# Clipped differences on GpSimd, a split scratch array in DRAM, and four projection banks beside three scan banks

## The chip, the cores and the metric

The kernel runs on one core of a Trainium2 chip. A core has TensorE (PE in the profile; its weight loads are PEld), VectorE (DVE), ScalarE (ACT), GpSimd (POOL) and SyncE (SP, which here only issues DMAs), each with its own queue that is worked off in order. They share an SBUF of 128 partitions; TensorE writes its products to the eight banks of PSUM, 2 KB a partition each. The metric is the device time of one execution in microseconds, the median of three runs.

## The reference, cut to what matters

Two layers of a streaming encoder run over 256 frames of a new stream and 64 frames of a running one, 320 columns in all. The first layer is a Mamba-2 mixer and a convolutional feed-forward block, the second an MLA mixer and another such block. The change touches the mixer of the first layer alone, and there the scan:

```python
da = dtc * a                                   # log decay of each step, 32 heads
acs = jnp.cumsum(da, axis=2)                   # running sums in a chunk
seg = acs[:, :, :, None] - acs[:, :, None]     # l minus s
decay = jnp.exp(jnp.where(causal, seg, -jnp.inf))
cb = jnp.einsum('bclgn,bcsgn->bclsg', cc, bc)
wts = cb[..., None] * decay * dtc[:, :, None]
y_diag = jnp.einsum('bclsge,bcsgep->bclgep', wts, xc)
decay_end = jnp.exp(acs[:, :, -1:] - acs)
states = jnp.einsum('bclgn,bclge,bclgep->bcgepn', bc, decay_end * dtc, xc)
chunk_decay = jnp.exp(acs[:, :, -1])
y_off = jnp.einsum('bclgn,bcgepn,bclge->bclgep', cc, h_prev, jnp.exp(acs))
```

`seg` is at most 0 where it is used (l at or behind s), since the running sums fall; elsewhere `cb` is set to zero.

## The kernel before

Activations lie transposed: features on the partitions, the 320 columns along a row. A projection is a sum over eight blocks of 128 input features, and each product is made of three matmuls (`mm3`, lines 283 and 284), since weights and inputs are split into a high part and a rest to keep float32 precision: ScalarE writes the high part of a weight tile `wh` (line 326), VectorE the rest `wl` (line 328). Weight tiles of 512 KB come in by SP through three buffers `wr` (line 191); four split pairs may stand ready.

The mixer's input projection is 41 output blocks of 128 rows. The first four (`outer`) are multiplied with the input not yet normalized; TensorE sums the squares meanwhile, VectorE makes 1/rms (`newton`), TensorE spreads it over the partitions (line 369), ScalarE copies it (`xr`, line 388), and the four results are multiplied with it as they are copied from PSUM (lines 818 and 642). Three more blocks are treated likewise, then GpSimd multiplies the input by 1/rms (`normalized`, line 478) and the rest is projected from that. Block results lie in PSUM tiles `pm`, from a pool `m` of five banks; the small products of the scan in `px`, from a pool `x` of two; sums of squares in `pr`, one bank (`PSM`, line 47).

A block is either a convolution block (b, c or x), copied to `ext` by ScalarE (line 640), with pads put in and last rows saved by GpSimd (lines 636, 637, 643, 644) and the filter on ScalarE and VectorE (lines 647, 649), or a gate block z, copied to `sz` (line 735).

The scan works in chunks of 128, 128 and 64 columns (c = 0, 1, 2) and four groups of eight heads (g). `ssm_dt` makes the running sums `acs`, 96 rows (32 heads in three chunks) of 128, and `ssm_dt2` stores them in DRAM as `acd` (line 841), to read them back spread over the partitions. For each group `ssd_fetch` issues per chunk a load of eight rows to all 128 partitions (`dc`, line 861) and, for c > 0, two loads of four rows to 64 partitions each (`ea`, line 866). Then come 24 steps `head(c, h)`: ScalarE replaces the row of head h by the clipped difference, a Relu of the column's own sum (from `dtt`) minus the row (line 874); the first step of chunks 1 and 2 also copies the sums' last column (`cd`, line 873). `ssd_decay` takes the exponentials of `cd`, `dc` and `ea` (line 673), with the sign turned for `dc`. `ssd_steps` makes the products: `pre` (b and c, lines 903 to 909: the mask, and `dc` times it), `xpose` (x turned, line 915, and times dt, line 922), `diag` (line 932 on `dc`, line 940 on the state, copied at line 934 or added up at 942 and 943) and `states` (line 949). Each takes one or two banks of `px`.

What sets the order: `PLAN` lists projections and scan parts in the order in which they are traced. `fetch` hands its 24 steps to a list from which a pace (6 or 8) is taken after each projection block, and `decay` works off what is left. Around that the framework's planner orders the instructions of each engine by a simulated timeline, first traced first where several are ready, and sets the semaphores; on the chip the order is fixed. Extra edges keep exponentials and silus apart on ScalarE (`exp` and `silu`), since each change of function loads a table, and put the loads of `acd` behind a projection block (`issue`). The last steps of the scan run beside the output projection (`square_part`), which holds four `pm` banks at a time.

Of the kernel before, what the change touches and what calls it, by code (L numbers as in the profile page):

```python
# [11 lines left out]
AF = mybir.ActivationFunctionType  # L12
ALU = mybir.AluOpType
# [3 lines left out]
P = 128  # L17
# [26 lines left out]
PSA = dict(m=5, x=3)  # L44
PSF = dict(m=7, r=1)
PSL = dict(m=7, r=1)
PSM = dict(m=5, x=2, r=1)
XC = ((0, 128), (128, 128), (259, 64))

RSU = 0.7235248917065753  # L50
# [35 lines left out]
class Kern:  # L86
# [513 lines left out]
    def run(self):  # L600
# [4 lines left out]
        self.pst = None  # L605
        self.psum(**PSM)
        self.vec = self.t(cp, [P, VEC["_n"][0]], "vec")
# [69 lines left out]
    def ssm(self):  # L677
        nc, a = self.nc, self.a
        self.silus, self.exps, self.burst = [], [], []
        self.yg, self.dc, self.ea = {}, {}, {}  # L680
        with ExitStack() as st:
            dr = st.enter_context(self.tc.tile_pool(name="acd", bufs=1, space=bass.MemoryType.DRAM))
            self.acd = self.t(dr, [96, P], "acd")
            ap = self.pool(st, "ssma")
            ah = self.t(ap, [P, 16, T], "ah", F32R)
            al = self.t(ap, [P, 16, T], "al", F32R)
            with ExitStack() as s2:
# [4 lines left out]
                with ExitStack() as s3:  # L692
# [3 lines left out]
                    for k in range(KD):  # L696
                        r = self.raw[k] = self.t(dp, [P, 512], "w0", bufs=KD)
# [76 lines left out]
            for half in range(2):  # L774
                w = [self.nextw(), self.nextw()]
                for n in range(4):
                    m = 4 * half + n
                    if m > 3:
                        self.early_step(early)
                    p = ps[3] if m == 7 else self.px()  # L780
                    for kb in range(12, 16):
# [4 lines left out]
                        q = slice((kb % 2 * 4 + n) * 128, (kb % 2 * 4 + n) * 128 + 128)  # L786
# [50 lines left out]
    def ssm_dt2(self, dt2, sp, dp):  # L837
        nc = self.nc
        dt, acs, w = dt2

        self.issue(nc.sync.dma_start(out=self.acd, in_=acs))
        self.cd = self.t(sp, [P, 3, 32], "cd")
        for p, n in ((slice(0, 64), 128), (slice(64, 96), 64)):
            self.exp(w[p, 0:n], acs[p, 0:n], scale=-1.0, bias=acs[p, n - 1:n])
        nc.vector.tensor_tensor(out=w, in0=w, in1=dt, op=ALU.mult)
        pd = self.px()
        for i, t_ in enumerate((dt, w, acs)):
            nc.tensor.transpose(pd[:, 96 * i:96 * i + 96], t_, self.ident[0:96, 0:96])
        self.dtt = self.t(sp, [P, 288], "dtt")
        nc.vector.tensor_copy(out=self.dtt, in_=pd[:, 0:288])  # L850

    def ssd_fetch(self, g, sp):

        nc = self.nc
        self.dc[g], self.ea[g] = {}, {}

        def load():
            for c, (_, n) in enumerate(CHUNKS):
                r0 = 32 * c + 8 * g
                dc = self.dc[g][c] = self.t(sp, [P, 8, n], f"dc{c}", bufs=DCB)  # L860
                self.issue(nc.sync.dma_start(out=dc, in_=self.acd[r0:r0 + 8, 0:n].partition_broadcast(P)))
                if c > 0:
                    ea = self.ea[g][c] = self.t(sp, [P, 4, n], f"ea{c}", bufs=DCB)
                    for odd in range(2):
                        r = r0 + 4 * odd
                        self.issue(nc.sync.dma_start(out=ea[64 * odd:64 * odd + 64], in_=self.acd[r:r + 4, 0:n].partition_broadcast(64)))

        def head(c, h):
            n = CHUNKS[c][1]
            dc = self.dc[g][c]  # L870
            q = 32 * c + 8 * g + h
            if c and h == 0:
                nc.vector.tensor_copy(out=self.cd[:, c, 8 * g:8 * g + 8].unsqueeze(2), in_=dc[:, :, n - 1:n])
            nc.scalar.activation(out=dc[:n, h, :], in_=dc[:n, h, :], func=AF.Relu, scale=-1.0, bias=self.dtt[:n, 192 + q:193 + q])  # L874

        return load, [lambda c=c, h=h: head(c, h) for c in range(3) for h in range(8)]

    def ssd_decay(self, g):

        cd = self.cd[:, 1:3, 8 * g:8 * g + 8]  # L880
        self.exp(cd, cd)
        for c, (_, n) in enumerate(CHUNKS):
            dc = self.dc[g][c]
            self.exp(dc[:n], dc[:n], scale=-1.0)
            if c > 0:
                self.exp(self.ea[g][c], self.ea[g][c])

# [624 lines left out]
```

## Time and profile before

| what | value |
|---|---|
| median of 3 runs | 1002.08 us (999.59 to 1002.16) |
| the profiled execution | 1002.07 us, span 1000.3 us |
| mean granted clock of TensorE | 0.983 |
| ScalarE, line 874 | 96 instructions, 28.3 us busy |
| loads `dc` / `ea` | 12 / 16 DMAs |
| the first layer's mixer | the first 260 us or so |

The span is the time from the first instruction to the last; the profiled execution's own time has 1.8 us around it. In rows of a timeline the columns are the start in us, the duration in us, engine, line, operation and operands (out<-in), how many instructions were merged, and in brackets the idle time before and what ended it. In rows of stretches the columns are the stretch, its length, each engine's busy time with the number of its instructions, the granted clock, the busy share of the DMA engines and GB/s. In rows for one line three numbers stand for the least, the median and the longest duration in ns. In rows of DMA issues the last two numbers are KB each and the median time from issue to landing in us.

### The profile page before, as it was taken

What the parts mean: (1) busy time and instruction counts of PE and PEld (TensorE: products, weight loads), DVE (VectorE), ACT (ScalarE), POOL (GpSimd) and SP (SyncE); (2) the same over time, 40 slices, a digit from 0 to 9 for tenths busy, and PEclk for the clock granted to TensorE, in tenths of its full rate; (3) what the DMA queues carried; (4) which work ended last, traced back from release to release, by engine and by line L of the source; (5) the groups of instructions that cost most, each with busy time, mean ns of one, the idle gap of its engine ahead of it and who ended that gap; (6) DMA issues with size and microseconds to landing.
All of it is one profiled execution on the core that took longest, in us unless ns stands there. A gap on an engine that the chain in (4) does not pass through costs nothing.

```text
span 1000.3 us, 18088 instructions
## 1 busy us (share of the span) xinstructions
PE 960.9 (96%) x6585; PEld 930.1 (93%) x6585; DVE 746.7 (75%) x1425; ACT 620.4 (62%) x1285; POOL 337.1 (34%) x597
## 2 busy tenths in 40 slices
PE   8897999999999999999999999999999999999995
PEld 7897999979989999999998899999999999999994
DVE  7865888887677998784538898886538999775433
ACT  6589797833555687664544677775544778664330
POOL 3921321100044775430005765530004766441001
PEclk9998999999999999999999999999999999999998
DMA  7374637353324444455641222233443455444531
GB/s 262 108 213 143 211 125 224 115 172 90 117 74 141 156 150 158 156 157 178 194 139 35 86 67 69 56 106 98 148 145 96 136 170 168 149 144 143 151 116 53
DMA packets 50905, 135.54 MB, mean 136 GB/s; under 512 B 11488, under 2 KB 15232, under 8 KB 50816
## 3 DMA queue, kind: packets, MB, share of 16 engines
q1 hardware_dynamic: 50528, 134.06, 42.6%
q8 instruction: 51, 0.84, 0.4%
q14 instruction: 38, 0.31, 0.1%
q10 hardware_dynamic: 288, 0.33, 0.1%
HBM read 130.25 MB, written 4.12 MB: 134 GB/s over the span
## 4 chain that ended last, share of the span: by engine, by line
PE 80%; DVE 9%; ACT 5%; POOL 3%; issue 2%; DMA 1%; SPq 0%; POOLq 0%; ACTq 0%; DVEq 0%
PE pm L283 46%; PE pm L284 23%; PE px L283 2%; PE px L932 1%; ACT wh L326 1%; PE px L949 1%; PE px L284 1%; POOL xacc L442 1%; PE pr L362 1%; PE px L940 1%; ACT dc L874 1%; DVE wl L328 1%; POOL xn L478 1%; DVE y L450 1%; DVE x L454 1%
## 5 line engine op out<-in xcount | busy, mean ns | idle before, releaser
L326 ACT ACTIVATE wh<-wr 128x1024 fp32r<-128x1024 f32 (+4 forms) x235 | 228.0, 973 | 160.0 <-PE pm L283 141.9
L328 DVE TENSOR_TENSOR wl<-wr,wh 128x1024 fp32r<-128x1024 f32 (+2 forms) x204 | 244.2, 1197 | 110.4 <-ACT wh L326 109.3
L283 PE MATMUL pm<-xnh,wh 128*128 128x320 f32 x784 | 243.4, 312 | 3.9 <-ACT xnh L329 3.2
L283 PE MATMUL pm<-xnl,wh 128*128 128x320 f32 x784 | 244.6, 312 | 0.3 <-DVE xnl L330 0.3
L284 PE MATMUL pm<-xnh,wl 128*128 128x320 f32 x784 | 243.4, 311 | 0.0
L283 PEld LDWEIGHTS pm<-xnh,wh 128*128 128x128 f32 x784 | 147.5, 189 | 6.5 <-ACT xnh L329 3.8
L284 PEld LDWEIGHTS pm<-xnh,wl 128*128 128x128 f32 x784 | 147.8, 189 | 1.7 <-issue 1.7
L283 PEld LDWEIGHTS pm<-xnl,wh 128*128 128x128 f32 x784 | 147.9, 189 | 1.3 <-issue 0.7
L283 PE MATMUL pm<-ah,wh 128*128 128x320 f32 x452 | 139.8, 311 | 1.7 <-ACT ah L329 1.7
L284 PE MATMUL pm<-ah,wl 128*128 128x320 f32 x452 | 140.6, 311 | 0.0
L283 PE MATMUL pm<-al,wh 128*128 128x320 f32 x452 | 140.4, 311 | 0.0
L649 DVE SCALAR_TENSOR_TENSOR cv<-ext,vec,cv 128x322 f32<-128x322 f32 x176 | 96.7, 563 | 5.4 <-ACT cv L647 3.0
L636 POOL MEMSET ext<- 128x2 f32 (+1 forms) x112 | 10.8, 98 | 245.9 <-DVE al L330 83.2
L643 POOL COPY fsave<-ext 128x2 f32<-128x2 f32 x88 | 72.5, 823 | 53.6 <-ACT ext L640 49.3
L283 PEld LDWEIGHTS pm<-ah,wh 128*128 128x128 f32 x452 | 84.7, 188 | 2.5 <-ACT ah L329 2.0
L283 PEld LDWEIGHTS pm<-al,wh 128*128 128x128 f32 x452 | 85.1, 188 | 1.0 <-issue 1.0
L284 PEld LDWEIGHTS pm<-ah,wl 128*128 128x128 f32 x452 | 85.1, 188 | 1.0 <-issue 1.0
L328 POOL TENSOR_TENSOR wl<-wr,wh 128x512 fp32r<-128x512 f32 (+2 forms) x31 | 43.6, 1424 | 102.3 <-ACT wh L326 100.9
L283 PE MATMUL pm<-xgl,wh 128*128 128x320 f32 x220 | 68.3, 314 | 1.0 <-DVE xgl L426 1.0
L284 PE MATMUL pm<-xgh,wl 128*128 128x320 f32 x220 | 68.2, 313 | 0.7 <-DVE wl L330 0.7
L283 PE MATMUL pm<-xgh,wh 128*128 128x320 f32 x220 | 62.5, 316 | 2.8 <-ACT wh L329 1.3
L647 ACT ACTIVATE cv<-ext,vec 128x322 f32<-128x322 f32 x88 | 57.1, 654 | 9.5 <-POOL ext L637 6.6
(395 smaller groups left out, 2132.4 us busy)
## 6 DMA issues: line engine op xcount, KB each, us to landing
wr<-w_up SPq DMA_DIRECT2D x76, 512.0 KB, 3.3
wr<-w_in SPq DMA_DIRECT2D x37, 512.0 KB, 3.7
wr<-w_dn SPq DMA_DIRECT2D x32, 512.0 KB, 3.6
wr<-w_out SPq DMA_DIRECT2D x16, 512.0 KB, 3.4
wr<-w_o SPq DMA_DIRECT2D x16, 512.0 KB, 3.4
wr<-w_up_k SPq DMA_DIRECT2D x16, 384.0 KB, 3.2
wr<-w_dn SPq DMA_DIRECT2D x16, 384.0 KB, 3.2
dc<-acd SPq DMA_DIRECT2D x8, 512.0 KB, 6.4
```

Source lines behind the costliest of these rows:

```text
L283: for i in (mm(out, wh, xh, start=first, stop=False), mm(out, wh, xl, start=False, stop=False), mm(out, wl, xh, start=False, stop=last)):
L284: mm(out, wl, xh, start=False, stop=last)):
L326: self.high_ins = nc.scalar.activation(out=hdst, in_=src, func=AF.Copy).ins
L328: return lambda: e.tensor_tensor(out=ldst, in0=src, in1=hdst.bitcast(F32), op=ALU.subtract)
L362: i = self.nc.tensor.matmul(ps[:, o + b:o + b + 1], acc[:, l0:l0 + 128], self.ones[:, 0:1], start=True, stop=True)
L442: nc.gpsimd.tensor_tensor(out=acc, in0=acc, in1=s, op=ALU.add)
L450: tt(out=yk, in0=yk, in1=r, op=ALU.mult)
L454: e.tensor_tensor(out=xk, in0=xk, in1=yk, op=ALU.add)
L636: nc.gpsimd.memset(ext[:, 0:m], 0.0)
L643: nc.gpsimd.tensor_copy(out=rows_out[:, 0, :], in_=ext[:, TP:TP + m])
L647: nc.scalar.activation(out=c, in_=ext[:, 0:n], func=AF.Identity, scale=w(0), bias=b)
L649: nc.vector.scalar_tensor_tensor(out=c, in0=ext[:, i:i + n], scalar=w(i), in1=c, op0=ALU.mult, op1=ALU.add)
```

## The change

Three edits. The difference of a head is made on GpSimd with one tensor_scalar (the row minus the column's own sum, then the minimum with zero) in place of the Relu on ScalarE; its sign is turned, so the exponential of `dc` takes no scale. The scratch array in DRAM becomes two: chunks 0 and 1 in 64 rows of 128, chunk 2 in 32 rows of 64, stored by two DMAs; each load reads its rows as one run and writes each partition's tile as one run. The pool `m` has four banks and the pool `x` three.

```diff
-PSM = dict(m=5, x=2, r=1)
+PSM = dict(m=4, x=3, r=1)
...
-            self.acd = self.t(dr, [96, P], "acd")
+            self.acd = self.t(dr, [64, P], "acd"), self.t(dr, [32, 64], "acd2")
...
-        self.issue(nc.sync.dma_start(out=self.acd, in_=acs))
+        self.issue(nc.sync.dma_start(out=self.acd[0], in_=acs[0:64]))
+        self.issue(nc.sync.dma_start(out=self.acd[1], in_=acs[64:96, 0:64]))
...
-                r0 = 32 * c + 8 * g
+                r0 = 32 * (c % 2) + 8 * g
+                src = lambda a, b, p, c=c: self.acd[c // 2][a:b].rearrange("r l -> (r l)").partition_broadcast(p)
                 dc = self.dc[g][c] = self.t(sp, [P, 8, n], f"dc{c}", bufs=DCB)
-                self.issue(nc.sync.dma_start(out=dc, in_=self.acd[r0:r0 + 8, 0:n].partition_broadcast(P)))
+                self.issue(nc.sync.dma_start(out=dc.rearrange("p h l -> p (h l)"), in_=src(r0, r0 + 8, P)))
                 if c > 0:
                     ea = self.ea[g][c] = self.t(sp, [P, 4, n], f"ea{c}", bufs=DCB)
-                    for odd in range(2):
-                        r = r0 + 4 * odd
-                        self.issue(nc.sync.dma_start(out=ea[64 * odd:64 * odd + 64], in_=self.acd[r:r + 4, 0:n].partition_broadcast(64)))
+                    for p, r in ((slice(0, 64), r0), (slice(64, 128), r0 + 4)):
+                        self.issue(nc.sync.dma_start(out=ea[p].rearrange("p h l -> p (h l)"), in_=src(r, r + 4, 64)))
...
-            nc.scalar.activation(out=dc[:n, h, :], in_=dc[:n, h, :], func=AF.Relu, scale=-1.0, bias=self.dtt[:n, 192 + q:193 + q])
+            nc.gpsimd.tensor_scalar(dc[:n, h, :], dc[:n, h, :], self.dtt[:n, 192 + q:193 + q], 0.0, op0=ALU.subtract, op1=ALU.min)
...
-            self.exp(dc[:n], dc[:n], scale=-1.0)
+            self.exp(dc[:n], dc[:n])
```

## The prediction

> **What bounds the kernel now.** I read the page first, for the share of each engine and the chain of waits, then the busy time by stretches over the first layer's scan, which is the only stage that the change touches, and then the order of work on each engine around the one place where TensorE stands still.
>
> ```profile
> span 1000.3 us, 18088 instructions
> PE 960.9 (96%) x6585; PEld 930.1 (93%) x6585; DVE 746.7 (75%) x1425; ACT 620.4 (62%) x1285; POOL 337.1 (34%) x597
> core 0: us, PE busy (x) PEld busy (x) DVE busy (x) ACT busy (x) POOL busy (x), PEclk, DMA share, GB/s
> 66.00:82.70 16.70, 16.70 (x120) 15.55 (x118) 8.02 (x15) 16.02 (x49) 1.91 (x8) 1.00 0.98 274
> 82.70:92.90 10.20, 5.03 (x31) 4.07 (x30) 4.63 (x8) 10.18 (x26) 1.89 (x4) 0.67 0.01 2
> 93.00:114.00 21.00, 21.00 (x149) 19.28 (x148) 20.10 (x34) 14.96 (x28) 6.24 (x14) 1.00 0.65 222
> 114.00:139.50 25.50, 25.50 (x184) 24.24 (x183) 23.17 (x43) 25.47 (x60) 7.18 (x16) 1.00 0.54 166
> 139.50:162.00 22.50, 22.50 (x175) 21.36 (x174) 17.24 (x27) 15.10 (x28) 3.42 (x10) 1.00 0.52 166
> 162.00:187.00 25.00, 25.00 (x174) 22.80 (x173) 22.13 (x46) 24.01 (x57) 4.51 (x8) 1.00 0.62 184
> ```
>
> TensorE bounds the whole (96% busy). In the scan it is full in every stretch but one: 82.7 to 92.9 us, where it is busy for half the time at 0.67 of its clock, ScalarE is busy throughout, and VectorE is mostly idle. That hole is what the change can win. The order of work there, TensorE and then ScalarE:
>
> ```profile
> 82.67 0.30 PE L284 MATMUL pm<-xnh,wl 128*128 128x320 f32 x1
> 86.67 1.11 PE L915 MATMUL px<-con,xs 128*128 128x128 f32 x4 [3.70 <-ACT yg L934]
> 89.25 1.98 PE L932 MATMUL px<-dc,xa 128*64 128x128 f32 x16 [1.47 <-DVE xa L922]
> 91.16 1.99 PE L940 MATMUL px<-ct,hp 128*128 128x128 f32 x8
> 92.89 0.41 PE L283 MATMUL pm<-xnh,wh 128*128 128x320 f32 x1
> ...
> 82.22 0.62 ACT L673 ACTIVATE dc<-dc 64x512 f32<-64x512 f32 x1
> 82.84 1.28 ACT L668 ACT_TABLE_LOAD   x1
> ...
> 86.04 0.57 ACT L934 ACTIVATE yg<-px 128x512 f32<-128x512 f32 x1
> ...
> 66.60:86.10 19.50, 10.26 (x35) 1.00 0.82 223
> 66.68 2.46 ACT L874 ACTIVATE dc<-dc,dtt 128x128 f32<-128x128 f32 x8 [2.32 <-DMA dc<-acd]
> ```
>
> The transposes (L915) need a scan bank; both are held, one until ScalarE's copy at 86.04 (L934), and that copy stands behind everything ScalarE was given since the first decay block landed at 66.68. Of those 19.5 us, 10.26 go to 35 head differences (L874; the row of that stretch is for this line alone). TensorE has nothing else in its order, and the pause also halves its clock, so the products after it run at half speed.
>
> **The hole, priced.** It lasts from 82.97 (82.67 + 0.30) to 92.89: 9.92 us. What TensorE must do in it takes, where the clock is full:
>
> ```profile
> 65.79 0.60 PE L915 MATMUL px<-con,xs 128*128 128x128 f32 x4
> 76.42 1.10 PE L932 MATMUL px<-dc,xa 128*64 128x128 f32 x16
> 143.95 1.05 PE L940 MATMUL px<-ct,hp 128*128 128x128 f32 x8
> ```
>
> 0.60 + 1.10 + 1.05 = 2.75 us, so 9.92 - 2.75 = 7.2 us can be won at most.
>
> **Part 1, differences to GpSimd.** 96 ScalarE instructions go (24 a group; 7.37 us in the row for L874 of 114 to 139.5 below), 96 GpSimd ones come. The trace has no such GpSimd operation. Nearest rows: one input, 64 columns, 236 ns at best; 3 columns, 177 ns at best; two inputs, 320 columns, 854 ns at best.
>
> ```profile
> 114.00:139.50 25.50, 7.37 (x24) 1.00 0.54 166
> L1126 POOL CAST cql<-cql x3: 236/236/1302, 553.8 to 554.7; 128x64 fp32r<-128x64 f32 x3
> L643 POOL COPY ssave<-ext x24: 177/188/5703, 27.7 to 177.3; 128x3 f32<-128x3 f32 x24
> L478 POOL TENSOR_TENSOR xn<-x,xr x24: 854/926/4117, 25.3 to 793.8; 128x320 f32<-128x320 f32 x24
> ```
>
> By the one-input rows a column costs (236 - 177)/61 = 0.97 ns, a head of 128 columns 0.30 us and of 64 columns 0.24 us: 16 x 0.30 + 8 x 0.24 = 6.7 us a group. By the two-input row (2.1 ns a column) 0.44 and 0.31: 9.5 us. The operation has one streamed input, so I take 7.5 us. The first group's heads then end about 66.7 + 7.5 = 74 us, and ScalarE, rid of 35 heads, finishes the exponentials some 6 to 8 us before 82.22; the silu table and the work up to the copy (82.84 to 86.61, 3.8 us) end by about 80, before TensorE asks at 82.67. So the wait of 3.70 us and the halved clock go. The wait of 1.47 us for the products with dt (L922) stays: VectorE starts them only behind L915, and a third bank doesn't shorten that. Won: 7.2 - 1.5 = 5.7 us.
>
> GpSimd's own queue is a new wait: the pads and saved rows of the convolutions (L636, L637, L643, L644) stand behind the heads, ScalarE's L647 waits for the pads, and the exponentials in ScalarE's queue for the last head, with the weight splits (L326) behind them. Worse, GpSimd gets little room where VectorE works without a pause:
>
> ```profile
> 28.35 5.70 POOL L643 COPY ssave<-ext 128x3 f32<-128x3 f32 x1
> ...
> 28.53 1.21 DVE L328 TENSOR_TENSOR wl<-wr,wh 128x1024 fp32r<-128x1024 f32 x1
> ...
> 33.93 0.54 DVE L649 SCALAR_TENSOR_TENSOR ct<-ext,vec,ct 128x323 f32<-128x323 f32 x1
> ```
>
> A copy of 0.18 us took 5.70, from 28.35 to 34.05, while VectorE ran through without a gap. For groups 2 and 3, 7.5 us of heads meet 25.5 - 23.17 = 2.3 and 25 - 22.13 = 2.9 us of VectorE's idle time, so 5.2 and 4.6 us are late or taken from VectorE. Each is followed by a looser stretch (139.5 to 162 leaves VectorE 5.3 us), so the cost lies between 0 and 9.8 us. I take 0.2, because the splits run ahead of TensorE (it waits for nothing in these rows) and can take a delay of a few us.
>
> The Trainium skill says why, in "SBUF — State Buffer", section "Who interferes with whom": a VectorE instruction with two SBUF inputs contends with a GpSimd instruction that reads SBUF, and whoever issues first holds the shared port. The copy of 5.70 us agrees. Read strictly the rule speaks against this part, and the last rival below is its case.
>
> **Part 2, sums in DRAM.** The text speaks of runs of 4 KB. The packets say that most of the rows are already joined:
>
> ```profile
> DMA packets 2624, 3.54 MB, mean 272 GB/s; under 512 B 1718, under 2 KB 1718, under 8 KB 2623
> ...
> dc<-acd SPq DMA_DIRECT2D x4, 256.0 KB, 7.5
> h<-h SPq DMA_DIRECT2D x4, 256.0 KB, 3.6
> ```
>
> The first row is of 61 to 74 us, when two groups' loads go out. Not one packet lies between 512 B and 2 KB, though a row of the array is 512 B: eight neighbouring full rows already travel as one run of 4 KB. Only chunk 2, with 64 of 128 columns, goes in 256 B pieces, and only it changes (to 2 KB, and 1 KB for its half blocks). It lands after 7.5 us; as fast as h0 of the same size, 3.6. That is up to 3.9 us sooner, but in the first group its heads run last, behind 5 us of others: 0. At worst its landing binds as now: 0. The second store is one more issue on SP, whose queue waits there anyway: 0.
>
> **Part 3, banks: four and three.** The third scan bank removes the same 3.70 us a second time, so it adds nothing to the sum, but it insures it. The lost projection bank costs earlier:
>
> ```profile
> 20.29 0.31 PE L283 MATMUL pm<-xgh,wh 128*128 128x320 f32 x1
> ...
> 23.81 0.49 PE L369 MATMUL pr<-con,rk 128*128 128x128 f32 x3
> ...
> 34.16 0.31 PE L283 MATMUL pm<-xnh,wh 128*128 128x320 f32 x1
> ...
> 34.90 0.31 PE L284 MATMUL pm<-xnh,wl 128*128 128x320 f32 x1
> ...
> 41.37 0.88 PE L283 MATMUL pm<-xnh,wh 128*128 128x320 f32 x3 [2.46 <-ACT xnh L329]
> 34.10:38.90 4.80, 4.02 (x26) 3.49 (x24) 3.29 (x8) 2.28 (x4) 4.36 (x4) 1.00 0.33 114
> 40.99 0.54 DVE L642 TENSOR_TENSOR ext<-pm,xr 128x256 f32<-128x256 f32 x2
> ```
>
> A projection matmul takes (34.90 - 34.16)/5 = 0.148 us, a block of 24 of them 3.5 us. Now one such block (20.29 to 23.81) fills the wait for rstd in the fifth bank, and the spread of rstd (L369) stands behind it. Without that bank the block comes behind the spread. If rstd is ready at once, the normalized input, for which TensorE waits at 41.37 (2.46 us), is there up to 3.5 us sooner; if it isn't, TensorE stands for as long with nothing to fill in: -3.5 to +3.5. From 34.1 to 38.9 two z blocks advance together (26 matmuls) while three banks wait for the copy of 40.99 and two later ones; with four banks one advances: 13 x 0.148 = 1.9 us is deferred. Later, a backlog of copies could hold one block once, 3.5 us. Bounds -3.5 and +8.9; I take +1.0, half of the row that I can count, since the other two can fall either way or not at all.
>
> **The sum**, against the profiled execution's own 1002.07 us (span 1000.3 and 1.8 around it; the median of the runs is 1002.08): -7.2 + 1.5 + 0.2 + 0 + 1.0 = -4.5, so 997.6 us.
>
> **The rivals.** First, the banks eat it: 1.9 + 3.5 instead of 1.0, so -7.2 + 1.5 + 0.2 + 5.4 = -0.1: 1002.0. For it: VectorE's late copies; against it: ScalarE's copies of projection blocks come sooner without the heads. Second, the change doesn't move the hole: the planner lays the products in TensorE's order by its own estimates, so it may put the first products (L932) earlier than the landing at 66.6 and the heads allow, and TensorE stands there as long: 1002.1. For it: today's order is already ahead of what ScalarE delivers; against it: there are 16 us of full projection work before the hole. Third, slower: heads on GpSimd are locked out by VectorE in the first group. The last exponential of the group then waits for GpSimd; the point from which this decides is (82.22 - 66.68)/24 = 0.65 us a head. The saved-row copies of 3 columns average:
>
> ```profile
> L643 POOL COPY ssave<-ext 128x3 f32<-128x3 f32 x24 | 15.8, 658 | 37.1 <-ACT ext L640 37.0
> ```
>
> 658 ns against 177 at best, 0.48 of waiting each; a head would take 0.30 + 0.48 = 0.78, 24 of them 18.7 us, 3.2 past that point: 1005.3. That is the page rule's case too. Against it: VectorE is busy for only 8.02 of the 16.7 us before the hole.
>
> **How the numbers follow.** Forecast 0.52, banks 0.16, planner 0.12, lock-out 0.20. 0.3% is 3.0 us, about what a measurement of this kernel can tell from no change: faster is below 999.1, slower above 1005.1. The forecast gives faster, less a little for its spread: 0.51; banks and planner with that spread give same: 0.28; lock-out gives slower, with a little from the banks' end: 0.21. The forecast's own range is 994.5 to 1000.5: the wait of 1.5 us gone too and the input 1.6 sooner, or 1.9 + 1.0 more for the z blocks and GpSimd. The full one starts where the hole goes wholly and the input comes 3.5 us sooner (1002.07 - 7.2 - 3.5 = 991.4) and ends where the banks cost all of 8.9 (1002.07 - 5.5 + 8.9 = 1005.5), just past the lock-out: 991.4 to 1005.5.
>
> **What would show it.** Right: L915's wait for L934 is gone, no half clock around 86 to 93, the last exponential of the first group before 78, every later stage some 5 us earlier. GpSimd's heads at 0.3 to 0.4 us: the price holds; at over 0.65: the third rival. A wait of projection matmuls for L642, L640 or L735 shows the fourth bank's price; unchanged 4 KB packets show that only chunk 2 moved. The forecast is wrong if a wait of 4 us or more stands on TensorE anywhere between 20 and 210 us.

## The result, and the profile after

The changed kernel takes 1006.70 us (median of 5 runs, 1006.13 to 1006.86) against 1002.08 (5 runs, 999.59 to 1003.12): a ratio of 1.005, 95% interval 1.0036 to 1.0065. It is slower by half a per cent, above the forecast and above the end of its range. The first lines of the page, after:

```profile
span 1004.6 us, 18134 instructions
PE 961.0 (96%) x6585; PEld 932.1 (93%) x6585; DVE 751.3 (75%) x1425; ACT 597.5 (59%) x1189; POOL 425.0 (42%) x693
```

ScalarE lost 22.9 us of work (620.4 before), GpSimd gained 87.9 (337.1 before). Where the time went shows in stretches of the first mixer; the kernel before first, then the changed one (columns as before: stretch, length, busy time of TensorE, its weight loads, VectorE, ScalarE, GpSimd, then the clock):

```profile
60.00:140.00 80.00, 74.83 (x523) 69.73 (x523) 61.86 (x108) 71.25 (x170) 20.37 (x48) 0.96 0.62 190
205.00:262.00 57.00, 54.71 (x391) 49.63 (x390) 43.65 (x80) 21.92 (x33) 0.61 (x6) 0.97 0.39 126
```

```profile
82.70:92.90 10.20, 10.20 (x73) 9.36 (x72) 6.80 (x10) 5.32 (x9) 10.20 (x12) 0.93 0.50 157
60.00:140.00 80.00, 67.00 (x454) 60.74 (x453) 59.44 (x104) 45.53 (x87) 72.82 (x109) 0.89 0.55 167
205.00:262.00 57.00, 57.00 (x416) 54.17 (x415) 43.79 (x74) 28.84 (x42) 2.65 (x6) 1.00 0.44 142
```

The hole of 82.7 to 92.9 us is filled, as forecast (10.20 of 10.20 where it was 5.03). But from 60 to 140 us, while GpSimd makes the heads of the first three groups, TensorE is busy 7.8 us less, at a lower clock, and GpSimd is busy for 72.82 us of 80. The end of the mixer, 205 to 262, is better than before. What GpSimd does in that time, and who stands behind it: GpSimd's timeline, two rows of ScalarE's and three of TensorE's in the changed kernel.

```profile
68.56 6.42 POOL L875 TENSOR_SCALAR dc<-dc,dtt 128x128 f32<-128x128 f32 x8 [4.06 <-DMA dc<-acd]
...
76.45 27.87 POOL L875 TENSOR_SCALAR dc<-dc,dtt 128x128 f32<-128x128 f32 x28
104.28 0.18 POOL L643 COPY ssave<-ext 128x3 f32<-128x3 f32 x1
104.40 0.18 POOL L644 COPY ssave<-ext 128x3 f32<-128x3 f32 x1
104.56 4.58 POOL L875 TENSOR_SCALAR dc<-dc,dtt 128x128 f32<-128x128 f32 x6
...
109.46 4.33 POOL L875 TENSOR_SCALAR dc<-dc,dtt 64x64 f32<-64x64 f32 x6
113.73 0.09 POOL L636 MEMSET ext<- 128x3 f32 x1
113.77 0.18 POOL L637 COPY ext<-vec 128x3 f32<-128x3 f32 x1
...
104.61 0.50 ACT L640 ACTIVATE ext<-pm 128x256 f32<-128x256 f32 x2 [6.20 <-POOL ssave L644]
113.99 0.66 ACT L647 ACTIVATE xs<-ext,vec 128x323 f32<-128x323 f32 x1 [3.98 <-POOL ext L637]
...
105.16 0.63 PE L283 MATMUL pm<-xnh,wh 128*128 128x320 f32 x1 [1.96 <-ACT ext L640]
120.36 0.47 PE L916 MATMUL px<-con,xs 128*128 128x128 f32 x1 [5.58 <-ACT xs L668]
124.08 2.08 PE L950 MATMUL px<-xa,bcs 128*128 128x512 f32 x2 [3.24 <-DVE xa L923]
```

Read it as a chain. From 68.56 to 113.79 GpSimd does hardly anything but the 48 heads of two groups. Two copies of three columns, 0.18 us each, wait in its queue until 104.28. They save the last rows of a convolution and hold its buffer, so ScalarE stands for 6.20 us before it may copy the next projection block (L640), and TensorE for 1.96 us. The pads of the next block come at 113.77; ScalarE stood for 3.98 us, then filters late, applies the silu late, and TensorE's transposes of x (L916) wait 5.58 us. The waits from 60 to 210 us, with their sum, their number and the longest:

```profile
ACT ext L640 <- POOL ssave L644: 9.7, 2, 6.2
ACT xs L647 <- POOL ext L637: 8.3, 2, 4.3
...
PE px L916 <- ACT xs L668: 5.6, 1, 5.6
ACT dc L673 <- POOL dc L875: 4.7, 2, 4.0
```

ScalarE waited 18.0 us for these copies and pads behind heads, and only 4.7 us for heads themselves. The price of a head (groups by form, and the least, median and longest of the first eleven and of those from 99 to 116 us):

```profile
L875 POOL TENSOR_SCALAR dc<-dc,dtt 128x128 f32<-128x128 f32 x64 | 66.0, 1047 | 4.7 <-DMA dc<-acd 4.6
L875 POOL TENSOR_SCALAR dc<-dc,dtt 64x64 f32<-64x64 f32 x32 | 23.6, 753 | 0.0
...
L875 POOL TENSOR_SCALAR dc<-dc,dtt x11: 709/715/2092, 68.6 to 79.5; 128x128 f32<-128x128 f32 x11
L875 POOL TENSOR_SCALAR dc<-dc,dtt x18: 491/703/2364, 99.2 to 115.8; 128x128 f32<-128x128 f32 x10, 64x64 f32<-64x64 f32 x8
```

Its least and most frequent time is 0.71 us for 128 columns and 0.49 for 64; the means are 1.05 and 0.75. In all 89.6 us, 22.4 a group, where 7.5 were forecast.

### The profile page after: what moved, and what is told of

The parts are those of the page before. It is cut to its first block, busy times and chain, and to the rows that moved or that the text cites. A ratio compares the mean times of both kernels' runs of the same rounds, so it can differ in the third digit from the quotient of the medians.

```text
span 1004.6 us, 18134 instructions
## 1 busy us (share of the span) xinstructions
PE 961.0 (96%) x6585; PEld 932.1 (93%) x6585; DVE 751.3 (75%) x1425; ACT 597.5 (59%) x1189; POOL 425.0 (42%) x693
## 4 chain that ended last, share of the span: by engine, by line
PE 72%; DVE 12%; POOL 7%; ACT 4%; issue 3%; DMA 2%; SPq 0%; ACTq 0%; POOLq 0%; DVEq 0%
PE pm L283 43%; PE pm L284 21%; POOL dc L875 4%; PE px L283 2%; DVE wl L328 2%; DVE xs L649 1%; ACT wh L326 1%; PE px L284 1%; POOL xacc L442 1%; PE pr L362 1%; PE px L950 1%; DMA wr<-w_in 1%; DVE cv L649 1%; PE px L933 1%; DVE xnl L330 1%
## 5 line engine op out<-in xcount | busy, mean ns | idle before, releaser
L875 POOL TENSOR_SCALAR dc<-dc,dtt 128x128 f32<-128x128 f32 (+1 forms) x96 | 89.4, 949 | 4.7 <-DMA dc<-acd 4.6
```

The costliest lines, as they stand in the source:

```text
L875: nc.gpsimd.tensor_scalar(dc[:n, h, :], dc[:n, h, :], self.dtt[:n, 192 + q:193 + q], 0.0, op0=ALU.subtract, op1=ALU.min)
```

## Experiments

All times are medians of repeated runs; the kernel before ran beside them on the same chips at medians of 1001.2 to 1002.1 (1002.0 beside the first four), and each median is known to some 1.5 us, so differences under 2 us between two kernels say little. "Small steps" are the zeroes, pads and two saved rows of the mixer's 24 convolutions (lines 636, 637, 643, 644), on GpSimd in both kernels of the case. The last two columns are TensorE's busy time and granted clock from 60 to 140 us and from 205 to 262 us.

| kernel | heads | small steps | banks | sums | us | of 80 | of 57 |
|---|---|---|---|---|---|---|---|
| before | ScalarE | GpSimd | 5/2 | one | 1002.0 | 74.83, 0.96 | 54.71, 0.97 |
| e1_heads | GpSimd | GpSimd | 5/2 | one | 1009.06 | 70.09, 0.91 | 56.71, 1.00 |
| e2_rows | ScalarE | GpSimd | 5/2 | split | 1011.82 | 75.88, 0.96 | 50.04, 0.85 |
| e9_two_stores | ScalarE | GpSimd | 5/2 | one | 1001.73 | 74.08, 0.94 | 54.71, 1.00 |
| g1_queue_alone | ScalarE | ScalarE | 5/2 | one | 1012.54 | 72.52, 0.96 | 49.00, 0.88 |
| f5_heads_queue | GpSimd | ScalarE | 5/2 | one | 1001.06 | 77.85, 1.00 | 53.18, 1.00 |
| e3_banks | ScalarE | GpSimd | 4/3 | one | 998.16 | 73.86, 0.96 | 57.00, 1.00 |
| h1_heads_banks | GpSimd | GpSimd | 4/3 | one | 1005.29 | 67.82, 0.91 | 57.00, 1.00 |
| g2_banks_queue | ScalarE | ScalarE | 4/3 | one | 999.14 | 74.97, 0.94 | 57.00, 1.00 |
| f2_no_rows | GpSimd | ScalarE | 4/3 | one | 995.81 | 74.74, 0.94 | 57.00, 1.00 |
| e4_no_heads | ScalarE | GpSimd | 4/3 | split | 1000.25 | 72.58, 0.96 | 57.00, 1.00 |
| after | GpSimd | GpSimd | 4/3 | split | 1006.70 | 67.00, 0.89 | 57.00, 1.00 |
| f1_queue_no_heads | ScalarE | ScalarE | 4/3 | split | 994.38 | 76.96, 0.94 | 57.00, 1.00 |
| e7_queue | GpSimd | ScalarE | 4/3 | split | 996.26 | 75.21, 0.98 | 57.00, 1.00 |
| f6_pads | GpSimd | pads on ScalarE | 4/3 | split | 1000.80 | 74.00, 0.98 | 57.00, 1.00 |
| g4_third | a third on GpSimd | ScalarE | 4/3 | split | 998.46 | 72.51, 0.98 | 57.00, 1.00 |
| e5_vector | VectorE | GpSimd | 4/3 | split | 1004.43 | 80.00, 1.00 | 48.21, 0.91 |
| h3_vector_queue | VectorE | ScalarE | 4/3 | split | 999.04 | 80.00, 1.00 | 50.33, 0.91 |
| e6_one_op | GpSimd, one step | GpSimd | 4/3 | split | 996.87 | 73.48, 1.00 | 57.00, 1.00 |
| g3_queue_one_op | GpSimd, one step | ScalarE | 4/3 | split | 991.43 | 77.50, 1.00 | 57.00, 1.00 |

### Each part alone

e1_heads is the kernel before with these two lines of the change:

```diff
-            nc.scalar.activation(out=dc[:n, h, :], in_=dc[:n, h, :], func=AF.Relu, scale=-1.0, bias=self.dtt[:n, 192 + q:193 + q])
+            nc.gpsimd.tensor_scalar(dc[:n, h, :], dc[:n, h, :], self.dtt[:n, 192 + q:193 + q], 0.0, op0=ALU.subtract, op1=ALU.min)
...
-            self.exp(dc[:n], dc[:n], scale=-1.0)
+            self.exp(dc[:n], dc[:n])
```

e2_rows has the split array with its stores and loads alone, as in the diff of the change; e3_banks only this:

```diff
-PSM = dict(m=5, x=2, r=1)
+PSM = dict(m=4, x=3, r=1)
```

and e4_no_heads is the changed kernel with the two lines of e1_heads undone.

> The kernel before with the heads on GpSimd alone (five and two banks, one scratch array). Theory, GpSimd's queue: the heads fill it (about 90 us for 96 heads, as in the profile of the change) and pads and saved rows of the convolutions stand behind them, so this alone is slower than before by 3 to 8 us, with ScalarE waiting for GpSimd at L640 and L647. Rival, the banks: the heads alone are harmless or win a part of the hole of 82.7 to 92.9 us, so -5 to +1 us. Rival, the planner's new order: anything, with no long wait on GpSimd.

> The kernel before with the split scratch array alone. All theories: within 2 us of before, since only chunk 2's pieces of 256 B change (to 2 KB and 1 KB); the loads of chunk 2 land in under 6 us, not 7.5. More than 3 us either way would mean that the order of the planner moved.

> The kernel before with four and three banks alone. Theory, GpSimd's queue: the wait of 3.70 us before the transposes goes, the wait of about 2.4 us for a projection bank near 24 us comes, so -4 to +1 us against before. Rival, the banks: slower than before by 3 us or more, with TensorE waiting for copies of projection blocks.

> The changed kernel with the heads back on ScalarE (split array, four and three banks). Theory, GpSimd's queue: the holes of 102 to 105 and 114 to 125 us go, 998 to 1002 us, 4 us or more under the changed kernel. Rival, the banks: as slow as the changed kernel, 1005 to 1008 us.

Measured, as ratios to the kernel before: heads 1.0064 (1.0052 to 1.0077), rows 1.0099 (1.0083 to 1.0114), banks 0.9967 (0.9953 to 0.998), all but the heads 0.9984 (0.9975 to 0.9994). The heads cost about 7 us alone and 6.4 beside the other two (1006.70 - 1000.25). The banks win 3.9. The split array was the surprise: 9.8 us alone, 2.1 beside four and three banks (1000.25 - 998.16). Along one path through the table the heads lead from 1002.0 to 1009.06 (+7.1), the banks to 1005.29 (-3.8), the array to 1006.70 (+1.4, within the spread).

### Why the split array costs 9.8 us alone

e9_two_stores splits only the store, into the one array of before:

```diff
-        self.issue(nc.sync.dma_start(out=self.acd, in_=acs))
+        self.issue(nc.sync.dma_start(out=self.acd[0:64], in_=acs[0:64]))
+        self.issue(nc.sync.dma_start(out=self.acd[64:96, 0:64], in_=acs[64:96, 0:64]))
```

> The kernel before with the store of the sums split in two, rows 0 to 63 and rows 64 to 96 of 64 columns, into the one array that it has; banks, heads and loads are those of before. Theory P, the 9.8 us that the split array cost alone is the planner's order, which any small change of the DMAs tips: 4 us or more away from 1002.0, to either side. Theory H, it is the loads in runs of 4 KB themselves: within 1 us of 1002.0.

1001.73 us, ratio 1.0005 (0.9995 to 1.0014): a second store costs nothing and leaves the order of the four compute engines as it was; theory P, that any small change of the DMAs tips it, falls. That leaves the loads, but not by what they take on the chip. Issues of the kernel before, where chunk 2 took 7.5 us as shown, and then of e2_rows:

```profile
dc<-acd SPq DMA_DIRECT2D x8, 512.0 KB, 6.4
```

```profile
dc<-acd SPq DMA_DIRECT2D x8, 512.0 KB, 5.8
dc<-acd SPq DMA_DIRECT2D x4, 256.0 KB, 6.6
```

By their medians the loads land sooner. The loss has its own place, the end of the mixer. TensorE's timeline of e2_rows there, and below it some rows of the kernel before:

```profile
216.36 0.31 PE L284 MATMUL pm<-ah,wl 128*128 128x320 f32 x1
216.60 1.12 PE L950 MATMUL px<-xa,bcs 64*128 64x512 f32 x2
...
220.11 1.12 PE L916 MATMUL px<-con,xs 128*128 128x128 f32 x4 [1.05 <-DVE bcs L908]
223.86 2.05 PE L950 MATMUL px<-xa,bcs 128*128 128x512 f32 x2 [2.64 <-DVE xa L923]
...
239.77 0.83 PE L283 MATMUL pm<-ah,wh 128*128 128x320 f32 x4
```

```profile
227.17 2.08 PE L940 MATMUL px<-ct,hp 128*128 128x128 f32 x8
228.90 0.61 PE L283 MATMUL pm<-al,wh 128*128 128x320 f32 x1
...
232.46 1.02 PE L949 MATMUL px<-xa,bcs 128*128 128x512 f32 x2
232.92 0.71 PE L284 MATMUL pm<-ah,wl 128*128 128x320 f32 x1
```

For 23.2 us, from 216.6 to 239.8, there is no projection matmul in e2_rows, only products of the last group, which wait for each other through VectorE, at a mean granted clock of 0.63. In the kernel before, projection matmuls lie among them. So the planner, given other loads, laid the last group's products in one row with nothing to fill their waits. With three banks the table shows 57.00 of 57 in that stretch for every kernel whose heads are not on VectorE; with two, 49 to 56.7. That the cost is the new order, and not the array as such, is argued from the sooner loads and from the place of the loss; no run of the kernel before with the split array holds the order fixed. One pair elsewhere comes near to it: the traces of h1_heads_banks and of the changed kernel, which differ in the array alone, show nearly the same order on every engine, and there the array costs 1.4 us, within the spread.

### What stands behind the heads

e7_queue is the changed kernel with the small steps on ScalarE, so that GpSimd's queue holds nothing behind the heads in that time; f6_pads moves only the first two.

```diff
-        nc.gpsimd.memset(ext[:, 0:m], 0.0)
-        nc.gpsimd.tensor_copy(out=ext[:, q:q + m], in_=pads)
+        if m == 3:
+            nc.scalar.activation(out=ext[:, 0:m], in_=pads, func=AF.Copy, scale=0.0)
+            nc.scalar.activation(out=ext[:, q:q + m], in_=pads, func=AF.Copy)
+        else:
...
-        nc.gpsimd.tensor_copy(out=rows_out[:, 0, :], in_=ext[:, TP:TP + m])
-        nc.gpsimd.tensor_copy(out=rows_out[:, 1, :], in_=ext[:, W - m:W])
+        for j, o in ((0, slice(TP, TP + m)), (1, slice(W - m, W))):
+            if m == 3:
+                nc.scalar.activation(out=rows_out[:, j, :], in_=ext[:, o], func=AF.Copy)
+            else:
...
```

> The changed kernel with the four small steps of each of the 24 mixer convolutions (zeroes, pads, two saved rows) on ScalarE in place of GpSimd, so that nothing stands behind the heads in GpSimd's queue but heads. Theory Q, the loss is the queue behind the heads (ScalarE waited 8.3 us for pads and 9.7 us for saved rows between 60 and 210 us): most of 6.4 us comes back, 999 to 1003, though ScalarE takes 96 steps of about 0.2 us. Theory D, the loss is the decay that ends late because its own heads end late (4.7 us of waits of the decay exponentials on heads): 1005 to 1008.

> The changed kernel with only the zeroes and pads of the mixer's convolutions on ScalarE; the saved rows stay on GpSimd behind the heads. ScalarE waited 8.3 us for pads and 9.7 us for saved rows in 60 to 210 us of the changed kernel. Theory both, each carries about half of the 10.4 us: 1000 to 1003. Theory pads, only the pads stand on the path (a convolution can't start without them, saved rows hold only the third buffer after): 995 to 998.5. Theory saved, the saved rows hold the buffer and with it the next copy out of PSUM: 1004 to 1007.

e7_queue: 996.26 us, ratio 0.9942 (0.9929 to 0.9954), 10.4 us faster than the changed kernel, 3 below what theory Q gave, and more than all the heads had cost. f6_pads: 1000.80, ratio 0.9987 (0.9976 to 0.9998), 5.9 us faster, so by the times pads and saved rows carry about half each, though ScalarE still waits 12.1 us for saved rows there. Theory D, the late decay, falls: in e7_queue the heads got dearer and ScalarE waited longer for them than in the changed kernel (14.5 us against 4.7), and it is 10.4 us faster. Groups and waits of e7_queue (lines are 7 further down):

```profile
L882 POOL TENSOR_SCALAR dc<-dc,dtt 128x128 f32<-128x128 f32 x64 | 82.9, 1312 | 49.6 <-DMA dc<-acd 49.6
L882 POOL TENSOR_SCALAR dc<-dc,dtt 64x64 f32<-64x64 f32 x32 | 20.5, 660 | 0.0
...
ACT dc L680 <- POOL dc L882: 14.5, 7, 3.5
```

Whether the small steps also pay without heads in front of them:

```diff
-            nc.gpsimd.tensor_scalar(dc[:n, h, :], dc[:n, h, :], self.dtt[:n, 192 + q:193 + q], 0.0, op0=ALU.subtract, op1=ALU.min)
+            nc.scalar.activation(out=dc[:n, h, :], in_=dc[:n, h, :], func=AF.Relu, scale=-1.0, bias=self.dtt[:n, 192 + q:193 + q])
```

is the difference of f1_queue_no_heads to e7_queue (and the sign of the exponential); g1_queue_alone is the kernel before with the small steps on ScalarE, g2_banks_queue that with four and three banks, f5_heads_queue the kernel before with the heads on GpSimd and the small steps on ScalarE, f2_no_rows is e7_queue with the one array, h1_heads_banks the kernel before with heads and banks.

> The kernel with the small convolution steps on ScalarE (996.26), and its head differences on ScalarE too, as in the kernel before; four and three banks and the split array stay. Theory Q, moving the small steps only pays because the heads stand in GpSimd's queue: with the heads off it the small steps gain nothing and ScalarE carries 96 heads (0.39 us each) and 96 small steps (about 0.2 us) more than GpSimd's version, so 1000 to 1005, at or above the 1000.25 of the same kernel with the small steps on GpSimd. Theory N, the small steps on ScalarE are a gain by themselves (a wait between two engines less in each convolution): 994 to 998.

> The kernel before with one edit: the small steps of the mixer's convolutions (zeroes, pads, saved rows) on ScalarE. Theory N, GpSimd's waits for VectorE's port make these steps late in any kernel (0.5 to 1.0 us each there against some 0.2 us on ScalarE): 3 to 6 us faster than before, 996 to 999. Theory B, ScalarE is what bounds 80 to 100 us of the kernel before (19 of 20 us busy), so 96 steps more on it make that hole longer: 1002 to 1006.

> The kernel before with two edits: four and three banks, and the small convolution steps on ScalarE; heads stay on ScalarE, the sums in one array. Theory add, the gains of the two (3.9 and 5.9 us) add: 991 to 994. Theory order, the split array's price changes with every kernel, so it may as well be worth something here: 994 to 997, at or above the 994.38 of the same kernel with the split array.

> The kernel before with two edits alone: heads on GpSimd, and the small convolution steps on ScalarE; five and two banks and one array stay. The prediction gave the heads alone a gain of 7.2 less 1.5, with the queue behind them at 0.2. Theory Q, the queue was the whole error: 995 to 999 (heads alone 1009.1). Theory K, two banks for the scan lose what the heads win: 1000 to 1005.

> The kernel with the small convolution steps on ScalarE, heads on GpSimd and four and three banks, but the sums in the one array of before. Theory R, the split array costs some 2 us beside four and three banks (1000.25 with it and without the heads, 998.16 for the banks alone): 993 to 995.5. Theory S, the array decides nothing but the planner's order, so that its price doesn't carry over from one kernel to the next: anywhere from 994 to 1000.

> The kernel before with two edits: heads on GpSimd, and four and three banks; the sums in one array, the small steps on GpSimd. Theory Q, the heads cost 6 to 7 us wherever the small steps stand behind them in GpSimd's queue, with either split of the banks and of the array: 998.2 and 6.4 to 7.1, so 1003.5 to 1006.5. Theory order, their price is the order that the planner happens to find: outside of that, below 1002 or above 1008.

f1_queue_no_heads: 994.38, ratio 0.9926 (0.991 to 0.9942), which contradicted theory Q as I had put it: the small steps won 5.9 us without the heads too. But g1_queue_alone is at 1012.54, 1.0107 (1.0089 to 1.0125), 10.5 us slower than before and worse than either theory had it, and g2_banks_queue at 999.14, 0.997 (0.9958 to 0.9982), 1.0 slower than the banks alone and above both ranges: theory N, a gain by itself, falls as well, and so does the theory that the gains add. f5_heads_queue: 1001.06, 0.9995 (0.9981 to 1.001), inside theory K; with two banks the end of the mixer keeps its gap (53.18 of 57). f2_no_rows: 995.81, 0.9937 (0.9922 to 0.9952), just above theory R and inside S; h1_heads_banks: 1005.29, 1.0038 (1.0024 to 1.0052), inside theory Q. Read as pairs:

| moving the small steps to ScalarE | heads on GpSimd | heads on ScalarE |
|---|---|---|
| 5/2, one array | 1009.06 to 1001.06: -8.0 | 1002.0 to 1012.54: +10.5 |
| 4/3, one array | 1005.29 to 995.81: -9.5 | 998.16 to 999.14: +1.0 |
| 4/3, split array | 1006.70 to 996.26: -10.4 | 1000.25 to 994.38: -5.9 |

With the heads on GpSimd the move pays 8 to 10 us each time; with the heads on ScalarE its sign changes from case to case. Read the other way, the heads on GpSimd cost 7.1, 7.1 and 6.4 us where the small steps stand behind them, and -11.5, -3.3 and +1.9 where they don't.

The traces show the mechanism behind the first three of these prices. Between 60 and 210 us ScalarE waits for small steps for 14.1 us in e1_heads, 17.9 in h1_heads_banks and 18.0 in the changed kernel; with the heads on ScalarE the same three kernels (before, e3_banks, e4_no_heads) show 0, 0 and 0.7. And from 60 to 140 us TensorE is busy for 4.7, 6.0 and 5.6 us less than in those three. The last two cases have nearly the same order, so they count for little more than one.

How much of the 8 to 10 us that the move pays is the queue, and how much a new order, isn't separated, since every such edit changes the order of all engines too. The other prices, from -11.5 to +1.9, aren't explained case by case. One of them shows its place: g1_queue_alone loses at the mixer's end like e2_rows.

```profile
205.00:262.00 57.00, 49.00 (x320) 41.74 (x319) 41.95 (x81) 17.00 (x25) 0.23 (x2) 0.88 0.31 98
```

### The price of a head, and other places for it

e6_one_op and g3_queue_one_op leave the subtraction out of the changed kernel's and of e7_queue's heads; g4_third gives GpSimd only chunk 2's heads; e5_vector and h3_vector_queue give all to VectorE (`nc.vector` in place of `nc.gpsimd`).

```diff
-            nc.gpsimd.tensor_scalar(dc[:n, h, :], dc[:n, h, :], self.dtt[:n, 192 + q:193 + q], 0.0, op0=ALU.subtract, op1=ALU.min)
+            nc.gpsimd.tensor_scalar(dc[:n, h, :], dc[:n, h, :], 0.0, None, op0=ALU.min)
```

> The changed kernel with each GpSimd head reduced to one step, a minimum with zero; the subtraction of the head's own sum is left out, so the decays are wrong in value and the work beside them is the same. Theory A1, the price is that of the two-step instruction with a per-row operand: one step comes at the forecast's 0.30 to 0.44 us for 128 columns, a group at 7 to 10 us, and the time at 998 to 1002. Theory A2, the price is that of any GpSimd pass over 128 columns, and being locked out by VectorE adds the rest: the mean stays above 0.75 us and the time above 1004.

> The kernel with heads on GpSimd and the small steps on ScalarE (996.26), each head reduced to a minimum with zero (the subtraction is left out, so the decays are wrong in value). Theory price, the heads' remaining 1.9 us are their length: with a cheaper instruction 993 to 995, at the 994.38 of the kernel with the heads on ScalarE or below. Theory place, what remains is the wait from engine to engine or the order: 995.5 to 998.

> The kernel with the small steps on ScalarE, four and three banks and the split array, where GpSimd takes only the last chunk's 8 of 24 head differences a group (64 columns, 0.5 to 0.9 us each) and ScalarE the other 16. Theory share, ScalarE is relieved of 8 x 0.33 us a group and GpSimd's 4 to 7 us end before the last chunk's decay is due: 992 to 994.4. Theory place, any head on GpSimd is late for the exponential on ScalarE: 995 to 998.

> The changed kernel with the 96 head differences on VectorE in place of GpSimd (same two-step instruction). Theory A, GpSimd is the wrong engine for them (0.71 us for 128 columns unblocked, 1.05 us with VectorE beside it): the GpSimd queue is free again and the heads cost VectorE a few us a group, so the time is at that of the kernel with the heads on ScalarE, 1000.25, or below: 996 to 1001. Theory B, any place but ScalarE gives the planner another order that happens to be bad: 1004 or above. Theory C, VectorE is the next bound in 80 to 140 us (15 to 17 us busy of 20 there): 1002 to 1005, with waits of TensorE on VectorE's decay products and head values in those stretches.

> The kernel with the small steps on ScalarE, three scan banks and the split array, its heads on VectorE (0.28 us for 128 columns, 0.24 for 64). Theory bound, VectorE has no room between 180 and 240 us, where it held the last group back with the small steps on GpSimd (1004.4): 1000 to 1005. Theory free, with ScalarE and GpSimd both unburdened the scan's products come in time: 991 to 995.

The groups of e6_one_op, with the least, median and longest of its heads, and TensorE's stretch:

```profile
L875 POOL TENSOR_SCALAR dc<-dc 128x128 f32<-128x128 f32 x64 | 53.1, 855 | 3.0 <-DMA dc<-acd 3.0
L875 POOL TENSOR_SCALAR dc<-dc 64x64 f32<-64x64 f32 x32 | 13.7, 455 | 0.0
L875 POOL TENSOR_SCALAR dc<-dc x96: 354/521/3918, 67.0 to 186.3; 128x128 f32<-128x128 f32 x64, 64x64 f32<-64x64 f32 x32
60.00:140.00 80.00, 73.48 (x538) 66.37 (x537) 67.01 (x118) 51.65 (x97) 56.66 (x120) 1.00 0.56 180
```

e6_one_op: 996.87 us, 0.9953 (0.9938 to 0.9969), 9.8 faster than the changed kernel. The step has means of 0.86 and 0.46 us: 66.8 us of heads instead of 89.6. Theory A2 had the mean right and the time wrong, A1 the time nearly right (1.1 too high) and the price wrong. The heads are a quarter shorter in sum and all of the loss is gone, but the shorter queue alone isn't shown to be why: the order of every engine is another too, and ScalarE still waits 10.4 us for small steps (18.0 in the changed kernel). g3_queue_one_op: 991.43, 0.9892 (0.9876 to 0.9909), 4.8 below e7_queue and below what theory price gave: either the length of a head counts also where nothing small stands behind it, or the order does; no run separates them.

On VectorE a head costs 0.28 and 0.24 us (e5_vector):

```profile
L875 DVE TENSOR_SCALAR dc<-dc,dtt 128x128 f32<-128x128 f32 x64 | 13.9, 278 | 1.1 <-DMA dc<-acd 1.1
L875 DVE TENSOR_SCALAR dc<-dc,dtt 64x64 f32<-64x64 f32 x32 | 6.0, 242 | 0.0
60.00:140.00 80.00, 80.00 (x582) 75.11 (x581) 75.87 (x181) 54.90 (x101) 29.09 (x48) 1.00 0.63 204
205.00:262.00 57.00, 48.21 (x332) 43.91 (x331) 41.21 (x72) 19.30 (x28) 0.61 (x6) 0.91 0.30 105
```

There TensorE is busy for all of the 80 us from 60 to 140, against 72.58 with the heads on ScalarE (e4_no_heads). And yet e5_vector is at 1004.43 (999.78 to 1010.00; ratio 1.0032, 1.0015 to 1.005), since 8.8 us of TensorE's time go at the mixer's end. Theory A falls; C has the time, but not the place that it named. h3_vector_queue: 999.04, 0.9974 (0.9964 to 0.9984), outside of both its theories, with the same full stretch and a like gap at the end (50.33 of 57). What makes the end late there wasn't settled. g4_third: 998.46, 0.9968 (0.9954 to 0.9982), worse than all heads on ScalarE (994.38) and, by little more than the spread, than all on GpSimd (996.26); theory place is nearer, but a late head alone can't make a third of them worse than all, so this stays open.

The best kernel that computes everything is f1_queue_no_heads, 994.38 us: banks, split array and small steps on ScalarE, with the heads left where they were. e7_queue is 1.9 us behind it, within the spread.

## Why the prediction was wrong

**The hole.** Right in its place: with the heads off ScalarE the wait of 3.70 us at L915 doesn't come back, and with the heads on VectorE the stretch has no gap. The third bank removes most of it too (8.66 busy of 10.20 in e3_banks), as the text said of this wait. But the gain of 5.7 us that the sum drew from it shows in no pair with three banks: even with the small steps out of the way the heads on GpSimd bring -3.3 and +1.9 us.

```profile
82.70:92.90 10.20, 8.66 (x76) 7.06 (x75) 7.62 (x14) 10.17 (x29) 1.01 (x3) 1.00 0.08 30
```

**The price of a head: mis-sized.** 0.30 to 0.44 us for 128 columns by the nearest rows; undelayed it is 0.71, so a group is 16 x 0.71 + 8 x 0.49 = 15.3 us instead of 7.5. Neither bound held. The nearest rows had one operation or two streams, not two operations with an operand per row, and from two sizes of different operations I drew a slope: 0.97 ns a column, where these heads show (0.71 - 0.49)/64 = 3.4. Time beside VectorE brings it to 22.4: in the changed kernel's trace the 17 of the 64 heads of 128 columns beside which VectorE worked for less than 30% of their time average 0.71 us, the 33 beside which it worked for over 95% average 1.23, though 12 of these took 0.71 as well. The first group's last exponential comes at 91.48, not before 78:

```profile
91.48 0.63 ACT L673 ACTIVATE dc<-dc 64x512 f32<-64x512 f32 x1 [4.00 <-POOL dc L875]
```

**GpSimd's queue: the step that failed.** The text named the pads and saved rows behind the heads, but bounded the cost of the queue, at 0 to 9.8, by the time that VectorE leaves GpSimd in groups 2 and 3, and took 0.2, "because the splits run ahead of TensorE (it waits for nothing in these rows) and can take a delay of a few us". What waits are not the splits alone but the copies out of PSUM and the filters, already in the first two groups, and the delay is not a few us: the saved rows stood behind 28 heads, 27.87 us. Part 1 was forecast at -5.7 + 0.2 = -5.5 us and costs 7.1 alone and 6.4 beside the other parts. Taking the small steps out gives back 10.4 us, but the same move gives 5.9 without heads in front, so 10.4 isn't the price of the queue alone. That the choice of 0.2 followed from the price of a head, since at 7.5 us a group the queue would have come free sooner, is argued; no run has heads of that price on GpSimd.

**DRAM rows: 0.** Right for the second store, and in the changed kernel the array costs 1.4 us, within the spread. Alone it costs 9.8, and the loss stands in TensorE's order at the end of the mixer. The sum had no term for a new order there.

**Banks: +1.0.** Wrong in sign: -3.9 by themselves (998.16) and -3.8 beside the heads (1009.06 to 1005.29). The cost that I looked for is there: a block that is still made of the input not normalized (`xgh`) has to wait 2.36 us, and no other block is left to fill that time. The profile puts it down to ScalarE in the changed kernel and, for the same wait in e3_banks (third row), to VectorE's copies out of PSUM (L818), which fits a lack of projection banks better.

```profile
23.70 0.31 PE L284 MATMUL pm<-xgh,wl 128*128 128x320 f32 x1
26.36 0.60 PE L283 MATMUL pm<-xgh,wh 128*128 128x320 f32 x1 [2.36 <-ACT xnh L329]
...
25.92 0.38 PE L283 MATMUL pm<-xgh,wh 128*128 128x320 f32 x1 [2.36 <-DVE v L818]
```

But the wait of 2.46 us for the normalized input shrinks to 0.30 in the changed kernel and 1.78 in e3_banks, and from 15 to 60 us TensorE is busy for 39.61 us before, 40.88 in the changed kernel and 39.41 in e3_banks, so the stage as a whole loses next to nothing. What I left out is the gain at 205 to 262, where the last group's products leave no gap. I priced the third scan bank only at the hole.

**The rivals.** The lock-out rival had the side and nearly the time (1005.3). Its point of decision, 0.65 us a head, was passed: the mean is 1.05 for 128 columns. Its mechanism, the last exponential that comes late, is a smaller part: ScalarE waited 4.7 us for heads and 18.0 for small steps behind them. Its price rested on heads of 0.30 and on waits of 0.48; the waits were of that size (1.05 - 0.71 = 0.34), the head itself not. The banks rival fell. The planner rival fell as it was put, since the hole is filled. That an order of the planner can cost as much elsewhere, at the last group's products, shows in e2_rows and g1_queue_alone, not in the changed kernel, whose last stretch is full. The text's own test, a wait of 4 us or more between 20 and 210, found the wait of 5.58 us at 120.36.

## What to carry to other kernels

Before work is moved to an idle engine, list what already stands in that engine's queue, who waits for it, and how long a run of the moved work will be: here ScalarE waited 18.0 us for copies of 0.18 us behind up to 28 such instructions, and the move cost 6 to 7 us where it was to win 5.5. An operation whose price no row shows should be taken at its dear bound, or beyond it, when its price decides another step's choice: here even the dear bound of 0.44 us was short of 0.71. And where a planner orders the engines by its own estimates, parts of a change need not add: their prices have to be read in pairs, and a single pair of times proves a mechanism only if the trace shows the place.

## What the runs showed of the hardware

A GpSimd step with two operations and an operand per row takes 0.71 us for 128 columns on 128 partitions and 0.49 for 64 on 64 where VectorE is mostly idle; with one operation and a constant 0.35 at least (64 columns) and 0.52 at the median of all; on VectorE the first takes 0.28. The Trainium skill's "GPSIMD Engine Reference", section "Engine selection", calls one-input work on GpSimd roughly line-rate beside VectorE; this step, with one streamed input, takes 2.6 times as long on GpSimd as on VectorE, so the measurement differs and decides. Single heads took up to 4.2 us, and the same heads averaged 1.05 us in one order of the work and 1.31 in another (e7_queue), so a mean from one kernel is no price for the next.
